# Freed activation tiles as buffers: three for gathered rows and four for weights in place of eight for weights

## The chip, the core and the metric

The kernel runs on one core of a Trainium2 chip. The metric is the device time of one execution in microseconds: 1776.36 us before the change, the median of 3 runs (1776.22 to 1776.38). A profile of one execution gives each instruction's time on the engines: PE (TensorE matmuls), PEld (its weight loads), DVE (VectorE), ACT (ScalarE), POOL (GpSimd) and SP, which issues most transfers.

## The reference

It is one layer of an encoder for two groups of tokens: 256 of a prompt and 128 (8 x 16) that are sampled, 1024 wide. A front part (modulation, projections, RWKV-7 and sparse attention, mixing) makes `x` and `h2`. What the change touches is the last part, a mixture of 16384 tiny experts:

```python
def block(hb):
    q = (hb @ w_pq).reshape(PEER_BLOCK, PEER_HEADS, 2, PEER_DHALF)
    ...
    e = jnp.take_along_axis(cidx, j, axis=-1)
    g = jax.nn.softmax(sc, axis=-1)
    act = jax.nn.gelu(jnp.einsum('nhkd,nd->nhk', peer_u[e], hb).astype(jnp.float32))
    return jnp.einsum('nhk,nhkd->nd', (g * act).astype(hb.dtype), peer_v[e])
```

For each token, 8 heads pick 16 experts each, so 128 of 16384. An expert is one row of `peer_u` and one row of `peer_v`, each 1024 floats. The output is `x + g2 * PEER(h2)`.

## The kernel before

The 128 sampled tokens go the **sparse** way (`peer_sparse`): one token per partition, and for each of its 128 experts one indirect DMA from POOL (L1593) gathers the rows u and v of that expert for all tokens, 128 x 2048 floats or 1 MB, into a row buffer. `ring` hands these buffers out, three of them (`EB = 3`, tag `raw`). DVE then multiplies u with h2 and sums to a dot product (L1600), ACT applies gelu and the weight (L1601, L1602), and DVE adds v times that to `acc` (L1606). The buffer is free after that.

The 256 prompt tokens go the **dense** way, over all 128 blocks of 128 experts. A key product (`dense_u`, accumulators `fx` and `mm`) makes gelu(h2 u), a tile of 128 experts x 256 tokens; for blocks 0 to 75 these stay in `G`, a tensor of 128 x 76 x 256 floats, for the others they are made during the next phase, a few ahead (`gA`) or by way of DRAM (`gO`, `gB`, L1522). They are multiplied by the routing weights (in `weights` for G, on POOL at L1528 for the others, with `Ws` from L1563). The last phase runs 128 value products (`dense_v`), numbered n from 0: each loads a 128 x 1024 block of `peer_v` (512 KB, `expert`, L1483), splits it into a high and a low part (`wh` on ACT at L233, `wl` on DVE at L237; likewise `Gh` and `Gl` for the tile of G) and adds twelve matmuls into the four accumulators `bx`, `cp`, `dx`, `dx` (L229); about every third product is done whole, without the split. Blocks below 76 and those above are interleaved by `order`.

While products run, the tiles of G that have been used are free. The kernel before appends one slot of four tiles (four tiles of 256 floats are one 1024-float weight buffer) to the queue of weight buffers after each of the blocks 3, 7, 11, ..., 31, so that it has four buffers at first and twelve at the end. Loads for key products use the same queue.

The sparse chain is drawn into this phase by `pull`: 0.62 of a gather per product, 55 gathers having been drawn in earlier phases. A gather also waits for its pace, the end of product n - 5. After product 122 what is left of the sparse chain is drawn, and the rows for the end are taken from the same ring: the gate (`gate2`, L1568, copied from a PE product) and the residual (`x1_rows`, L1581). `residual` multiplies the result by the gate and adds the residual (L1576, L1577), and L1578 stores it. It runs for the sampled tokens on `acc` and twice for the prompt on the four accumulators, after `finish_v` has done the last two products bank by bank.

The order of instructions on each engine is set by a scheduler when the program is built: it plans the program on a timeline of its own and puts the instructions of each engine in the order of that plan. On the chip each engine takes its instructions in that order, and each waits for what it reads and for the buffer that it writes.

Of the kernel before, what the change touches and what calls it, by code (L numbers as in the profile page):

```python
# [183 lines left out]
S0, PH = 30, 4  # L184
OFF = [j for j in range(NW, 128) if (j - NW + 1) * NB // (128 - NW) > (j - NW) * NB // (128 - NW)]
AHEAD = sorted(OFF + [j for j in range(NW, 128) if j not in OFF][:NA - 1])
LAST, EARLY, SLOTS = 126, 108, 8
WB, EB = (4, 4, 3), 3
UENG, VENG, GENG, VN = 'v', 'v', 'g', 3
SENG = 'gv'  # L190
# [7 lines left out]
class K:  # L198
    def __init__(self, ctx, tc, I, O):
        self.ctx, self.tc, self.nc, self.I, self.O = ctx, tc, tc.nc, I, O  # L200
        self.uid = 0
        self.const = self.open(ctx, "const")
        self.stream = self.open(ctx, "stream")
        self.dram = self.open(ctx, "dram", space=bass.MemoryType.DRAM)
        self.nlo = 0
        self.slots = deque([None] * WB[0])
        self.lo_pattern = "v"

    def open(self, ctx, name, **kw):
# [1259 lines left out]

    def ring(self):  # L1470

        r = self.t([128, 2048], tag="raw", bufs=EB, pool=self.peer)
        return r[:, :1024], r[:, 1024:]

    def expert(self, src):

        s = self.slots.popleft()
        self.slots.append(s)
        if s is None:
            w = self.t([128, 1024], tag="w", bufs=WB[0], pool=self.stream)  # L1480
        else:
            w = self.G[:, 4 * s:4 * s + 4].rearrange("p a b -> p (a b)")
        self.nc.sync.dma_start(w, src)  # L1483
        return w

# [124 lines left out]
    def run(self):  # L1610
# [79 lines left out]
        def pull(rate):  # L1690
            sn[0] += rate
            while sn[0] >= 1:
                sn[0] -= 1
                next(sparse, None)
# [46 lines left out]
        for n, j in enumerate(order):  # L1741
            self.pace = self.vdone[n - 5] if n > 4 else None
            pull(SR[2])
            while todo and sum(u not in OFF for u in gs) < NA - 1:
                u = todo.pop(0)
                gs[u] = self.dense_u(u)
            last.append(self.dense_v(j, gs.pop(j) if j >= NW else self.G[:, j], out, n))
            if j < 4 * SLOTS and j % 4 == 3:
                self.slots.append(j // 4)
            if n == 122:  # L1750
                for _ in sparse:
                    pass
                (a, b), (y, _) = self.ring(), self.ring()
                self.residual(0, [self.acc[:, c * 512:c * 512 + 512] for c in range(2)], self.gate2(0, a), self.x1_rows(0, b), y)
                (a, b), (c, y1), (y2, _) = (self.ring() for _ in range(3))
                g, x1, y = self.gate2(1, a), [self.x1_rows(1, b), self.x1_rows(2, c)], (y1, y2)
# [28 lines left out]
```

## Time and profile before

| | before |
|---|---|
| median of the runs | 1776.36 us |
| profiled execution, its time | 1775.95 us |
| its span | 1773.9 us |
| PE busy | 1664.8 us, 94% |
| DVE busy | 1354.5 us, 76% |
| gathers, POOL, L1593 | 128, 177.3 us busy, 501.9 us idle before them |
| gather, issue to landing | 8.3 us (median) |
| value products on PE | 1278 to 1718 us |
| moved in all | 437.22 MB, 246 GB/s |

The span runs from the first to the last instruction, and the execution's own time lies around it. A busy time is a sum over the span; what a stage is limited by is read from that stage. In the rows of groups, the idle time stands behind the busy time and the mean of one instruction, with the instruction that ended most of it. A row of waits names who waited, for whom, for how long in all, how many times, and the longest.

### The profile page before, as it was taken

Reading aid. Unit: us, or ns where it says so; the run is one execution under the profiler, and the core shown is the slowest. Engines: PE = TensorE matmul, PEld = TensorE weight load, DVE = VectorE, ACT = ScalarE, POOL = GpSimd, SP = SyncE. Lnnn points to the kernel's source line nnn. Section 1 sums busy time; section 2 is a strip of 40 time slices with the busy share of each in tenths; the row PEclk is TensorE's granted clock in tenths of the full one; section 3 lists DMA queues with packets and bytes.
Section 4 is the critical chain, followed back from the end, with each engine's and each line's share of the span. In section 5 each row is a group of like instructions: output and inputs, shape, how many; then the busy total and the mean of one; then the engine's idle time right before and its main releaser. Section 6 shows DMA issues by size and latency. Waiting matters only on the chain. (4 is left out here: it accounts for less than half of the span.)

```text
span 1773.9 us, 33227 instructions
## 1 busy us (share of the span) xinstructions
PE 1664.8 (94%) x12376; PEld 1412.1 (80%) x12376; DVE 1354.5 (76%) x2905; ACT 750.9 (42%) x1666; POOL 549.8 (31%) x621
## 2 busy tenths in 40 slices
PE   6999999999999988999999989999999999999970
PEld 4898788878878866998887889999876777777750
DVE  4449788878768845566999998999766676777896
ACT  4533433333333233444222365678733343434531
POOL 2434243333332310034123223431233123223332
PEclk8999999999999999999999999999999999999995
DMA  8543752463364276655598989986499989999957
GB/s 296 164 141 99 214 173 72 157 202 110 102 220 143 79 260 209 211 177 187 188 374 322 347 326 390 381 296 203 168 377 404 357 331 360 338 343 338 333 211 258
DMA packets 173049, 437.22 MB, mean 246 GB/s; under 512 B 46036, under 2 KB 86612, under 8 KB 156504
## 3 DMA queue, kind: packets, MB, share of 16 engines
q1 hardware_dynamic: 154456, 300.89, 50.2%
q0 software_dynamic: 18432, 134.23, 20.0%
q8 instruction: 97, 1.59, 0.4%
q14 instruction: 64, 0.52, 0.1%
HBM read 403.75 MB, written 31.30 MB: 245 GB/s over the span
## 5 line engine op out<-in xcount | busy, mean ns | idle before, releaser
L1593 POOL DMA_INDIRECT raw<-in_puv,pe x128 | 177.3, 1385 | 501.9 <-DVE acc L1606 319.7
L237 DVE TENSOR_TENSOR wl<-w,wh 128x1024 fp32r<-128x1024 f32 x208 | 261.1, 1260 | 91.8 <-ACT wh L233 35.3
L233 ACT ACTIVATE wh<-w 128x1024 fp32r<-128x1024 f32 x216 | 226.9, 1053 | 152.0 <-PE mm L229 71.0
L229 PE MATMUL fx<-h2h,wh 128*128 128x256 f32 x688 | 196.5, 286 | 0.2 <-ACT G L1509 0.2
L229 PE MATMUL fx<-h2h,wl 128*128 128x256 f32 x688 | 193.9, 283 | 2.1 <-DVE wl L237 2.1
L229 PE MATMUL fx<-h2l,wh 128*128 128x256 f32 x688 | 193.6, 282 | 0.0
L1606 DVE SCALAR_TENSOR_TENSOR acc<-raw,dots,acc 128x1024 f32<-128x1024 f32 x127 | 163.5, 1287 | 21.4 <-ACT dots L1602 20.6
L1600 DVE SCALAR_TENSOR_TENSOR raw<-raw,sh 128x1024 f32<-128x1024 f32 x128 | 159.8, 1249 | 15.2 <-DMA raw<-in_puv,pe 15.1
L229 PEld LDWEIGHTS fx<-h2h,wl 128*128 128x128 f32 x688 | 130.0, 189 | 3.7 <-DVE wl L237 3.1
L229 PEld LDWEIGHTS fx<-h2h,wh 128*128 128x128 f32 x688 | 129.9, 189 | 2.5 <-issue 1.2
L229 PEld LDWEIGHTS fx<-h2l,wh 128*128 128x128 f32 x688 | 129.7, 189 | 2.2 <-issue 1.7
L229 PE MATMUL mm<-LTh,wh 128*128 128x384 f32 (+2 forms) x352 | 123.7, 352 | 1.4 <-ACT wh L233 0.8
L229 PE MATMUL mm<-LTl,wh 128*128 128x384 f32 (+2 forms) x352 | 122.1, 347 | 1.4 <-POOL LTl L490 1.4
L229 PE MATMUL mm<-LTh,wl 128*128 128x384 f32 (+2 forms) x352 | 122.5, 348 | 0.0
L237 DVE TENSOR_TENSOR wl<-G,wh 128x1024 fp32r<-128x1024 f32 x66 | 84.9, 1288 | 47.3 <-issue 29.2
L1601 ACT ACTIVATE dots<-dots 128x1 f32<-128x1 f32 x128 | 25.4, 198 | 193.5 <-DVE raw L1600 193.4
L229 PE MATMUL mm<-h2f,w 128*128 128x256 f32 x464 | 105.4, 381 | 0.0
L229 PE MATMUL mm<-wh,LTh 128*128 128x256 f32 x336 | 99.0, 295 | 1.9 <-ACT qx L893 1.9
L229 PE MATMUL mm<-wl,LTh 128*128 128x256 f32 x336 | 100.0, 298 | 0.0
L229 PE MATMUL mm<-wh,LTl 128*128 128x256 f32 x336 | 98.7, 294 | 0.0
L229 PEld LDWEIGHTS mm<-h2f,w 128*128 128x128 f32 x464 | 87.5, 190 | 12.4
L229 PE MATMUL fx<-h2f,w 128*128 128x256 f32 x336 | 78.1, 385 | 0.0
(604 smaller groups left out, 4375.4 us busy)
## 6 DMA issues: line engine op xcount, KB each, us to landing
w<-in_puT SPq DMA_DIRECT2D x118, 512.0 KB, 6.7
G<-in_pv SPq DMA_DIRECT2D x74, 512.0 KB, 5.9
w<-in_w_in SPq DMA_DIRECT2D x70, 512.0 KB, 4.5
w<-in_pv SPq DMA_DIRECT2D x54, 512.0 KB, 6.2
w<-in_w_ada SPq DMA_DIRECT2D x48, 512.0 KB, 4.7
cKT<-in_cKT SPq DMA_DIRECT2D x32, 256.0 KB, 4.1
cV<-in_cV SPq DMA_DIRECT2D x32, 256.0 KB, 4.0
w<-in_w_pq SPq DMA_DIRECT2D x16, 512.0 KB, 3.7
```

The costliest lines, as they stand in the source:

```text
L229: return self.nc.tensor.matmul(out, l, r, start=start, stop=stop, skip_group_check=True, **kw)
L233: self.nc.scalar.activation(hi, src, AF.Copy)
L237: (self.nc.vector if eng == "v" else self.nc.gpsimd).tensor_tensor(lo, src, hi, op=OP.subtract)
L1593: d = nc.gpsimd.indirect_dma_start(out=bass.AP(tensor=u.tensor, offset=u.offset, ap=[u.ap[0], [1, 2048]]), out_offset=None, in_=self.I["puv"],
L1600: nc.vector.scalar_tensor_tensor(u, u, 1.0, h2, op0=OP.mult, op1=OP.mult, accum_out=dot)
L1601: nc.scalar.activation(dot, dot, AF.Gelu_apprx_tanh)
L1606: nc.vector.scalar_tensor_tensor(acc, v, dot, acc, op0=OP.mult, op1=OP.add)
```

## The change

A table `FREED` says after which block which tiles of G become free, and as what. The letters are taken in turn: R is a row buffer of eight tiles (2048 floats), W is a weight buffer of four. So after block 7 tiles 0 to 7 become a fourth row buffer, after block 11 tiles 8 to 11 a fifth weight buffer, after 19 the next row buffer (12 to 19), then 23 (W), 31 (R), 35 (W) and 39 (W). In the order of the value products these are numbers 9, 16, 30, 36, 50, 57 and 63. At the end there are six row buffers (before: three) and eight weight buffers (before: twelve). `ring` hands out its buffers from a queue, as `expert` did already.

```diff
-LAST, EARLY, SLOTS = 126, 108, 8
+LAST, EARLY = 126, 108
+FREED = {}
+for _k in "RWRWRWW":
+    _a = max((j + 1 for j in FREED), default=0)
+    FREED[_a + (7 if _k == "R" else 3)] = (_k, _a)
...
         self.slots = deque([None] * WB[0])
+        self.rslots = deque([None] * EB)
...
     def ring(self):
 
-        r = self.t([128, 2048], tag="raw", bufs=EB, pool=self.peer)
+        s = self.rslots.popleft()
+        self.rslots.append(s)
+        if s is None:
+            r = self.t([128, 2048], tag="raw", bufs=EB, pool=self.peer)
+        else:
+            r = self.G[:, s:s + 8].rearrange("p a b -> p (a b)")
         return r[:, :1024], r[:, 1024:]
...
-            w = self.G[:, 4 * s:4 * s + 4].rearrange("p a b -> p (a b)")
+            w = self.G[:, s:s + 4].rearrange("p a b -> p (a b)")
...
-            if j < 4 * SLOTS and j % 4 == 3:
-                self.slots.append(j // 4)
+            if j in FREED:
+                kind, a = FREED[j]
+                (self.slots if kind == "W" else self.rslots).append(a)
```

The buffers move the scheduler's plan, and so the order on the engines. The lines of the new kernel are 5 to 11 higher: its gather is at L1603, the dot product at L1610, the accumulation at L1616, the split at L242. A name's number grows in the order in which the program makes its tiles, so that a small number beside a large one is work drawn early and done late. A tile in G carries the number of G itself; its dot product then tells which gather it is.

POOL, in the middle of the phase, where gathers (L1593) stand among the multiplications of key tiles by routing weights (L1528), before:

```order
L1593 DMA raw_16925<-in_puv,pe_2107_10741 128x2048
L1593 DMA raw_16991<-in_puv,pe_2107_10741 128x2048
L1528 TENSOR_TENSOR gA_17118<-gA_17118,Ws_17931 128x256
L1528 TENSOR_TENSOR gA_17257<-gA_17257,Ws_17931 128x256
L1593 DMA raw_17020<-in_puv,pe_2107_10741 128x2048
L1528 TENSOR_TENSOR gB_17659<-gB_17659,Ws_17661 128x256
```

and now, around the same multiplications:

```order
L1603 DMA raw_17376<-in_puv,pe_2107_10741 128x2048
L1603 DMA raw_17409<-in_puv,pe_2107_10741 128x2048
L1603 DMA raw_17443<-in_puv,pe_2107_10741 128x2048
L1538 TENSOR_TENSOR gA_17127<-gA_17127,Ws_17936 128x256
L1538 TENSOR_TENSOR gA_17264<-gA_17264,Ws_17936 128x256
L1603 DMA G_11076<-in_puv,pe_2107_10741 128x2048
L1538 TENSOR_TENSOR gB_17666<-gB_17666,Ws_17668 128x256
```

Ahead of the same tile gB there stood gather 17020, and there stands now one after 17443: gathers are planned some 13 products earlier against the dense work.

DVE, early in the phase, dot products (L1600) and splits (L237) before:

```order
L1600 SCALAR_TENSOR_TENSOR raw_15768,dots_15770<-raw_15768,sh_2289_11699 128x1024
L237 TENSOR_TENSOR wl_15928<-w_15924,wh_15927 128x1024
L1606 SCALAR_TENSOR_TENSOR acc_11701<-raw_15768,dots_15770,acc_11701 128x1024
L237 TENSOR_TENSOR wl_15972<-G_11076,wh_15971 128x1024
L237 TENSOR_TENSOR Gl_16003<-G_11076,Gh_16002 128x256
```

and now:

```order
L1610 SCALAR_TENSOR_TENSOR raw_15966,dots_15968<-raw_15966,sh_2289_11699 128x1024
L242 TENSOR_TENSOR wl_16003<-w_16000,wh_16002 128x1024
L1616 SCALAR_TENSOR_TENSOR acc_11701<-raw_15966,dots_15968,acc_11701 128x1024
L242 TENSOR_TENSOR wl_16040<-w_16036,wh_16039 128x1024
L242 TENSOR_TENSOR Gl_16103<-G_11076,Gh_16102 128x256
```

A dot product stood 158 numbers ahead of the split behind it, five products; it now stands beside the split of the product with which it was drawn. Later in the phase the distance before grows to 31 products, and now it is two to five.

DVE, at the end of the phase, around the last splits, before:

```order
L237 TENSOR_TENSOR wl_18754<-G_11076,wh_18753 128x1024
L237 TENSOR_TENSOR Gl_18761<-gB_18757,Gh_18760 128x256
L1606 SCALAR_TENSOR_TENSOR acc_11701<-raw_17979,dots_17981,acc_11701 128x1024
L1600 SCALAR_TENSOR_TENSOR raw_18046,dots_18048<-raw_18046,sh_2289_11699 128x1024
L1606 SCALAR_TENSOR_TENSOR acc_11701<-raw_18046,dots_18048,acc_11701 128x1024
```

and now:

```order
L1610 SCALAR_TENSOR_TENSOR G_11076,dots_18511<-G_11076,sh_2289_11699 128x1024
L242 TENSOR_TENSOR Gl_18683<-gA_17894,Gh_18682 128x256
L242 TENSOR_TENSOR wl_18606<-w_18603,wh_18605 128x1024
L1616 SCALAR_TENSOR_TENSOR acc_11701<-G_11076,dots_18511,acc_11701 128x1024
L1586 TENSOR_TENSOR G_11076<-acc_11701,G_11076 128x512 x2
L242 TENSOR_TENSOR wl_18631<-w_18628,wh_18630 128x1024
```

Before, the last split (18754) had 13 more dot products behind it. Now the dot product of the last gather (18511, drawn with product 117) stands ahead of the last seven splits, and its accumulation and the sampled tokens' residual (L1586) ahead of six.

## The prediction

> **What bounds the kernel now.** I read the table by stages first, over the last 488 us, in which the value products run (columns: PE, PEld, DVE, ACT and POOL busy us, granted clock, DMA share, GB/s).
>
> ```profile
> 1286.00:1320.00 34.00, 34.00 (x156) 25.93 (x155) 21.17 (x26) 12.70 (x25) 14.92 (x16) 1.00 0.99 370
> 1320.00:1360.00 40.00, 38.57 (x163) 26.88 (x162) 30.51 (x37) 16.57 (x32) 12.29 (x10) 1.00 1.03 404
> 1360.00:1400.00 40.00, 40.00 (x190) 30.40 (x189) 27.23 (x35) 15.79 (x31) 9.31 (x9) 1.00 0.96 361
> 1400.00:1500.00 100.00, 100.00 (x441) 72.51 (x439) 69.23 (x82) 39.89 (x76) 26.02 (x24) 1.00 0.94 353
> 1500.00:1600.00 100.00, 100.00 (x445) 73.36 (x444) 70.86 (x82) 39.68 (x75) 30.95 (x25) 1.00 0.94 338
> 1600.00:1700.00 100.00, 100.00 (x422) 75.65 (x421) 83.02 (x99) 47.73 (x87) 35.39 (x25) 1.00 0.84 308
> 1700.00:1718.00 18.00, 18.00 (x77) 14.09 (x76) 16.60 (x21) 6.41 (x15) 6.05 (x5) 1.00 0.65 232
> 1718.00:1754.00 36.00, 0.29 (x2) 0.00 (x0) 25.39 (x31) 5.44 (x21) 14.54 (x10) 0.54 0.83 293
> ```
>
> Up to 1718 us PE is full, at full clock, and the transfers nearly so. Then PE is empty for 36 us. The rows of time show its first value product, its last, what ends the pause, and the last adds and stores.
>
> ```profile
> 1278.13 2.81 PE L229 MATMUL bx<-w,G 128*128 128x512 f32 x6
> 1717.90 0.39 PE L229 MATMUL dx<-wh,Gl 128*128 128x512 f32 x1
> 1754.18 3.78 PE L229 MATMUL fx<-modr,clate 128*128 128x512 f32 x4 [35.89 <-ACT raw L1568]
> 1767.06 1.29 DVE L1576 TENSOR_TENSOR raw<-dx,raw 128x512 f32<-128x512 f32 x2
> 1769.13 1.29 DVE L1577 TENSOR_TENSOR raw<-raw,raw 128x512 f32<-128x512 f32 x2 [0.77 <-DMA raw<-d]
> ```
>
> The chain of waits over that tail is made of gathers:
>
> ```profile
> 1717.96 10.36 DMA raw<-in_puv,pe x2
> 1728.76 8.23 DMA raw<-in_puv,pe
> 1737.08 6.58 DMA raw<-in_puv,pe
> 1750.65 6.45 DMA raw<-in_puv,pe
> 1759.67 1.30 DVE acc L1606
> 1765.15 3.88 DMA raw<-d
> ```
>
> The issues between 1718 and 1758 us and, from the waits between 1286 and 1700 us, why they come so late:
>
> ```profile
> raw<-in_puv,pe POOLq DMA_INDIRECT x10, 6.3
> ...
> POOL raw L1593 <- DVE acc L1606: 191.9, 35, 9.7
> POOL raw L1593 <- PE dx L229: 42.8, 9, 6.9
> PE bx L229 <- ACT wh L233: 1.0, 1, 1.0
> ```
>
> Ten of the 128 gathers are issued after PE's last product. While PE worked, POOL stood 191.9 us because none of three row buffers was free, against 42.8 us for the pace (product n-5). PE itself waited 1.0 us. So two limits share the end: PE to 1718.3 us (1717.90 + 0.39), then a sparse chain that is late for want of buffers.
>
> **The change part by part.** *Arithmetic.* No product, gather or load is added, and no duration should move: what is a buffer in G is 128 partitions of the same size as before. Cost 0.
>
> *Three more row buffers.* They remove the wait on acc. In the new order the dot product of a gather stands beside the split of the weights pulled with it, and the last accumulation stands ahead of the last splits; before it stood behind them. The tail of gathers then lies beside PE's work. If PE isn't slowed, what stands behind its last product is one multiplication, one addition and the store. The first two are 1.29 / 2 each by the two DVE rows; the add ends at 1769.13 + 1.29 = 1770.42 and the span at 1773.9, so the store and the close take 3.5 us. With 0.3 us for hand-overs (chosen, below the gap of 0.77 us in the last row) the tail is 0.65 + 0.65 + 3.5 + 0.3 = 5.1 us. The lower end of the span is 1718.3 + 5.1 = 1723.4 us. The gate and residual rows for it were also late (3.88 us for raw<-d) because they use the same buffers; the new order has them ahead of the last splits, covered by the same products. Without that cover, 3.9 us more.
>
> *What the transfers must carry.* This is the term that decides. By the table, 370 x 34 + 404 x 40 + 361 x 40 + 353 x 100 + 338 x 100 + 308 x 100 + 232 x 18 + 293 x 36 us make 158 MB from 1286 us to the last gather. About 2 MB of it (four loads of 512 KB) may follow the last gather, so 156 MB must have moved before it. In the new order the dot product of the last gather (pulled with product 117) stands ahead of the split of product 121, so seven products follow it. A product is twelve matmuls at 0.227 us, two such halves:
>
> ```profile
> 1701.57 1.36 PE dx L229 x6
> 1706.03 1.38 PE dx L229 x6
> ```
>
> that is 2.72 us, 19 us for seven, and 3 us for the dot product and the split between landing and PE. PE's end is thus the later of 1718.3 and 1286 + 156 MB / rate + 22 us:
> - at 404 GB/s, reached for 40 us in 1320:1360, the last gather lands at 1672 us: PE isn't slowed;
> - at 345 GB/s, the mean of 1400 to 1600 us as it is, 452 us: PE ends at 1760, slowed by 42 us;
> - at 368 GB/s, the same 345 divided by its share of 0.94, 424 us: PE ends at 1732, slowed by 14 us.
>
> I take the third: three more requests in flight fill the idle 6%, and these are the rows of the same mix of loads. The ends stay for the range. The pause in 1320:1360 gives the same size by another way: PE lost 1.4 of 40 us with the queues full, which over 390 us of full queues is 14 us.
>
> The Trainium skill, "DMA: Bandwidth & Descriptors", section "Specifications", gives about 358 GB/s of HBM per core. By that, an estimate from its figure, PE would end at 1744 us, 26 us slowed, and the kernel at 1752. The row with 404 GB/s over 40 us disagrees with it as a ceiling, so it stays inside my range.
>
> *Four weight buffers fewer at the end, eight in place of twelve in all, and later.* The fifth comes after product 16 (before: 3), the eighth after 63. With four, the fp32 key products before 1020 us kept PE at 96 to 97% full at 3.0 us a load:
>
> ```profile
> 800.00:900.00 100.00, 97.60 (x572) 85.79 (x572) 87.08 (x399) 35.42 (x72) 28.83 (x27) 0.98 0.62 210
> 900.00:1000.00 100.00, 96.48 (x451) 84.13 (x450) 98.60 (x382) 30.75 (x81) 27.85 (x24) 0.97 0.92 349
> ```
>
> A value product takes (1718.3 - 1278.1) / 128 = 3.4 us with the key products between, so four buffers cost at most 3.5% of the 55 us to product 16, 2 us. That is the upper end; the lower is 0, as the first loads now queue behind fewer others. I count it within the 14.
>
> **The sum.** 1718.3 + 14 + 5.1 = 1737.4 us of span. The profiled execution has 1775.95 us for a span of 1773.9, 2.05 around it, and the median of the runs is 0.41 above that execution: 1737.4 + 2.05 + 0.41 = 1740 us.
>
> **The rivals.** *A: the transfers go no faster than before.* The 345 GB/s could be what this mix gives. For it: share 0.94 already, and landing times in the crowded stretch (below). Against it: 404 GB/s. PE ends at 1760, the kernel at 1760 + 5.1 + 2.5 = 1768 us.
>
> *B: weights starve.* From the issues of 1286:1320, 1320:1350 and the queues of 1320:1360 and 1300:1700:
>
> ```profile
> w<-in_pv SPq DMA_DIRECT2D x7, 512.0 KB, 11.2
> raw<-in_puv,pe POOLq DMA_INDIRECT x6, 9.2
> ...
> G<-in_pv SPq DMA_DIRECT2D x4, 512.0 KB, 13.2
> ...
> q1 hardware_dynamic: 3521, 8.78, 57.7%
> q0 software_dynamic: 1008, 7.34, 44.8%
> ...
> q1 hardware_dynamic: 34477, 81.02, 55.4%
> q0 software_dynamic: 7856, 57.15, 37.2%
> ```
>
> Gathers move as packets of 57.15 MB / 7856 = 7.3 KB, the rest as 2.35 KB. If a full gather queue took half of the packets, it would take 76% of the bytes, some 303 of 400 GB/s, and leave 97 where 81.02 MB / 400 us = 203 are needed. Each 1.05 MB gather would then set PE back by 3.46 us x 106 / 203 = 1.8 us where no loads are ahead: 22 gathers to product 36 (0.62 a product, at most five weight buffers), 40 us, and the kernel at 1780. Against it: in 1320:1360 with both queues full the gathers had 7.34 of 16.1 MB, 45%, and PE lost 1.4 us. The Trainium skill, same page, section "Queues, rings and completion order", says that an engine goes round its queues packet by packet; the 45% is less than that rule would give, though three buffers may not have kept the queue full.
>
> *C, the slower side: the dot products hold up the splits.* DVE takes its work in order. The new order puts the dot product of a gather pulled with product n right ahead of the split of product n to n+2 (before, up to 31 products later), and the gather may not start before product n-5 is done. From the groups between 1286 and 1718 us:
>
> ```profile
> L1606 DVE SCALAR_TENSOR_TENSOR acc<-raw,dots,acc 128x1024 f32<-128x1024 f32 x58 | 74.7, 1287 | 14.9 <-ACT dots L1602 14.5
> L1600 DVE SCALAR_TENSOR_TENSOR raw<-raw,sh 128x1024 f32<-128x1024 f32 x58 | 73.9, 1274 | 0.5 <-DMA raw<-in_puv,pe 0.5
> L237 DVE TENSOR_TENSOR wl<-w,wh 128x1024 fp32r<-128x1024 f32 x44 | 57.4, 1304 | 30.8 <-PE dx L229 10.7 <-ACT wh L233 10.2 <-issue 6.9
> ```
>
> Where the split is that of product n, landing, dot product (1.27), split (1.30) and some 0.5 of hand-over must fit into four products, 13.8 us, so landing may take 10.7 us. The gathers' 9.2 us fits; the weights' 13.2 us would not. At a landing of 14 us each round of four products loses 3.3 us, 58 / 4 = 14.5 rounds up to product 58 lose 48, and the kernel ends at 1740 + 48 = 1788 us. It decides from 13.2 us on (36 us of gain / 14.5 rounds = 2.5 us). Behind the waiting dot product on DVE stand split and Gl of the next product, and PE waits for both. Against it: DVE waited 0.5 us for gathers at L1600, with the queues as full as in the second row.
>
> *D: the gathers aren't earlier.* If the pace were the limit, buffers would change nothing: 1776 us. For it are the 42.8 us, against it the 191.9.
>
> **How the numbers follow.** Forecast 0.73 (1740; its own range 1725 to 1758), A 0.13 (1768), B 0.04 (1780), C 0.06 (1788), D 0.04 (1776). The range 1725 to 1770 holds the forecast's cases but for its edges, and A. A measurement of this kernel tells 0.2%, 3.6 us, from no change. Faster: forecast and A, 0.86. Slower: B and C, 0.10. Same: D, 0.04.
>
> **What would show it.** Right: PE's pause of 35.89 us is gone, the last gather is issued before PE's last product, POOL's wait on acc falls far below 191.9 us, and the DMA share between 1400 and 1700 us rises to 0.97 or more. The 14 us would stand as waits of PE or of ACT and DVE on w, G or raw loads. PE's end at 1718 means the transfers had room to spare; one at 1745 or later with a share still near 0.94 means A; weight landings above 13 us with waits of wh on loads in the first 100 us mean B; a large wait of L1610 (L1600 before) on its gather, with PE waiting for wl, means C. The prediction is wrong if PE's value products end after 1750 us, or if a new wait stands behind their end.

## The result, and the profile after

| | before | after |
|---|---|---|
| median of the runs | 1776.37 us (6 runs, 1772.91 to 1777.25) | 1747.84 us (6 runs, 1745.32 to 1751.29) |
| profiled execution, its span | 1775.95, 1773.9 us | 1751.29, 1749.5 us |
| value products, first start to last end | 1278.1 to 1718.3 us, 440.2 | 1280.7 to 1744.7 us, 463.9 |
| last product to the end of the span | 55.6 us | 4.8 us |

The time after is 0.9842 of that before (95% interval 0.9828 to 0.9857), 28 us less. The forecast was 1740. The profiled execution is the slowest of the six, so sums made against it stand 3.5 us above the median.

The stages of the changed kernel (columns as in the first rows of the prediction):

```profile
1286.00:1320.00 34.00, 32.74 (x144) 23.22 (x142) 16.64 (x23) 10.52 (x22) 13.97 (x14) 1.00 0.93 346
1320.00:1360.00 40.00, 35.77 (x151) 24.29 (x151) 32.27 (x37) 16.04 (x33) 15.74 (x11) 1.00 0.96 365
1360.00:1400.00 40.00, 40.00 (x173) 28.80 (x171) 32.18 (x38) 16.06 (x32) 12.26 (x10) 1.00 1.01 381
1400.00:1500.00 100.00, 98.82 (x437) 71.68 (x436) 79.57 (x94) 38.89 (x81) 38.03 (x30) 1.00 1.00 381
1500.00:1600.00 100.00, 99.40 (x441) 72.59 (x440) 77.93 (x91) 39.15 (x81) 31.24 (x26) 1.00 1.00 385
1600.00:1700.00 100.00, 96.88 (x397) 68.59 (x395) 80.56 (x96) 41.67 (x84) 37.02 (x30) 1.00 0.98 376
1700.00:1718.00 18.00, 16.22 (x64) 12.62 (x63) 16.83 (x22) 8.85 (x18) 1.18 (x1) 0.91 0.77 267
1718.00:1735.00 17.00, 14.12 (x59) 10.39 (x58) 15.37 (x17) 8.82 (x16) 4.77 (x3) 1.00 0.15 58
...
1280.74:1744.68 463.94, 448.31 (x1913) 322.68 (x1912) 358.32 (x421) 183.48 (x371) 155.59 (x126) 1.00 0.92 349
```

The transfers are full from 1360 to 1700 us, at 376 to 385 GB/s where they had 308 to 361, and almost done by 1718, where before they ran on to the end. PE is no longer quite full: it was idle 2.0 of 440.2 us, and is idle 463.94 - 448.31 = 15.6 us. By the rows, 5.5 us of that lie between 1286 and 1360 us, only 1.8 us in the 240 us from 1360 to 1600 with full transfers, 3.1 us in the next 100, and 4.7 us between 1700 and 1735, where the transfers run out (a share of 0.77, then 0.15). Its busy time is 10 us longer too.

The rows of time, with the last gather, its dot product, the last value product and the last addition:

```profile
1280.74 2.81 PE L234 MATMUL bx<-w,G 128*128 128x512 f32 x6
1693.07 0.94 POOL L1603 DMA_INDIRECT G<-in_puv,pe  x1 [1.66 <-PE dx L234]
1720.49 1.22 DVE L1610 SCALAR_TENSOR_TENSOR G<-G,sh 128x1024 f32<-128x1024 f32 x1
1744.29 0.39 PE L234 MATMUL dx<-wh,Gl 128*128 128x512 f32 x1
1745.44 0.69 DVE L1587 TENSOR_TENSOR raw<-raw,raw 128x512 f32<-128x512 f32 x1
```

The pause of 35.89 us is gone, and the last gather is issued 51.6 us ahead of PE's end, where ten were issued behind it. The waits of POOL, of PE and of DVE's dot products during the value products:

```profile
POOL raw L1603 <- PE dx L234: 110.0, 31, 8.7
POOL G L1603 <- PE dx L234: 62.8, 18, 6.4
POOL G L1603 <- DVE acc L1616: 20.3, 5, 6.5
...
PE bx L234 <- ACT wh L238: 7.9, 8, 1.8
PE bx L234 <- DVE wl L242: 3.6, 4, 1.7
PE bx L234 <- DMA w<-in_pv: 1.7, 1, 1.7
...
DVE raw L1610 <- DMA raw<-in_puv,pe: 0.5, 1, 0.5
```

POOL's wait for a buffer (acc) fell from 204.2 us over the same stage (191.9 from 1286 to 1700 us) to 20.3, and its wait for the pace rose from 42.8 to 172.8. Further waits of its gathers are put down to other instructions of DVE (splits and dot products): 31.4 us now, 5.9 before. PE now waits for splits, 11.5 us in these rows and 1.5 us in the key products between, against 1.4 us before.

### The profile page after: what moved, and what is told of

Read it like the earlier page. It is cut to its first block, busy times and chain, and to the rows that moved or that the text cites. A ratio compares the mean times of both kernels' runs of the same rounds, so it can differ in the third digit from the quotient of the medians.

```text
span 1749.5 us, 33109 instructions
## 1 busy us (share of the span) xinstructions
PE 1671.5 (96%) x12376; PEld 1411.1 (81%) x12376; DVE 1358.9 (78%) x2905; ACT 744.2 (43%) x1666; POOL 550.2 (31%) x621
## 4 chain that ended last, share of the span: by engine, by line
PE 63%; DVE 17%; DMA 8%; issue 6%; ACT 3%; POOL 2%; SPq 0%; DVEq 0%; POOLq 0%; ACTq 0%
PE mm L234 23%; PE fx L234 12%; PE dx L234 11%; PE cp L234 7%; PE bx L234 7%; DVE acc L1616 2%; DVE wl L242 2%; DMA raw<-in_puv,pe 2%; DVE raw L1610 2%; DMA w<-in_w_in 1%; ACT wh L238 1%; DMA w<-in_puT 1%; POOL raw L1603 1%; DMA w<-in_pv 1%; DVE ps L1331 1%
## 5 line engine op out<-in xcount | busy, mean ns | idle before, releaser
L242 DVE TENSOR_TENSOR wl<-w,wh 128x1024 fp32r<-128x1024 f32 x231 | 291.5, 1266 | 94.3 <-ACT wh L238 55.3
L238 ACT ACTIVATE wh<-w 128x1024 fp32r<-128x1024 f32 x239 | 250.3, 1051 | 156.7 <-PE mm L234 70.9
L1603 POOL DMA_INDIRECT raw<-in_puv,pe x100 | 136.0, 1360 | 335.9 <-DVE acc L1616 118.0
L1616 DVE SCALAR_TENSOR_TENSOR acc<-raw,dots,acc 128x1024 f32<-128x1024 f32 x99 | 129.4, 1307 | 8.6 <-ACT dots L1612 8.5
L1610 DVE SCALAR_TENSOR_TENSOR raw<-raw,sh 128x1024 f32<-128x1024 f32 x100 | 125.4, 1254 | 7.4 <-DMA raw<-in_puv,pe 7.2
L234 PEld LDWEIGHTS mm<-LTh,wh 128*128 128x128 f32 (+2 forms) x352 | 66.7, 189 | 7.6 <-ACT wh L238 2.9
```

Source lines behind the costliest of these rows:

```text
L234: return self.nc.tensor.matmul(out, l, r, start=start, stop=stop, skip_group_check=True, **kw)
L238: self.nc.scalar.activation(hi, src, AF.Copy)
L242: (self.nc.vector if eng == "v" else self.nc.gpsimd).tensor_tensor(lo, src, hi, op=OP.subtract)
L1603: d = nc.gpsimd.indirect_dma_start(out=bass.AP(tensor=u.tensor, offset=u.offset, ap=[u.ap[0], [1, 2048]]), out_offset=None, in_=self.I["puv"],
L1610: nc.vector.scalar_tensor_tensor(u, u, 1.0, h2, op0=OP.mult, op1=OP.mult, accum_out=dot)
L1616: nc.vector.scalar_tensor_tensor(acc, v, dot, acc, op0=OP.mult, op1=OP.add)
```

## The experiments

Each kernel is the changed one with one edit, timed beside the kernel before on the same chip. Ratios are to that, with 95% intervals.

### The two halves apart

*Row buffers alone* and *weight buffers alone*: one kind is dropped from the table.

```diff
+FREED = {j: f for j, f in FREED.items() if f[0] == "R"}   # rows only
+FREED = {j: f for j, f in FREED.items() if f[0] == "W"}   # weights only
```

> The three row buffers stay, the four freed weight buffers are left unused: four weight buffers all through, as before product 16. Row theory (the gain is the tail of gathers that moves beside PE): the pause of 36 us stays away, so the time is clearly below 1776. If PE's loss of some 24 us in the value products comes from crowded transfers that make loads late, it must grow when only four loads can be ahead: 1758 to 1772 us. If it comes from the order on DVE and ACT at the start and at the end instead, four buffers suffice and it stays at 1746 to 1755.

> The four weight buffers stay, the three row buffers are left unused. Row theory: the gathers wait for acc again, the pause of 36 us on PE comes back and the time is 1774 to 1778 us, as before, with eight weight buffers in place of twelve. Rival (the gain came from the smaller lead of the weights, which left transfers to the gathers): a good part of it stays, 1750 to 1765 us.

Rows alone: 1753.44 us (1750.90 to 1756.24), ratio 0.9869 [0.9843, 0.9896]. Weights alone: 1763.92 us (1757.43 to 1768.16), ratio 0.9916 [0.9886, 0.9945]. The second has three row buffers, as before, and four weight buffers in place of eight, and yet gains 12 us. In its profile the pause (a row of time) and POOL's wait on acc are smaller, not gone (53.2 us more are put down to splits):

```profile
1748.37 3.78 PE L235 MATMUL fx<-modr,clate 128*128 128x512 f32 x4 [16.31 <-ACT raw L1579]
```

```profile
POOL raw L1604 <- DVE acc L1617: 121.8, 24, 12.0
POOL raw L1604 <- PE dx L235: 99.9, 24, 9.9
```

Fewer weight buffers alone had shortened a wait that I had put down to the number of row buffers. So the next run gave G's tiles to nobody.

*No added buffer at all*: four weight and three row buffers all through.

```diff
-for _k in "RWRWRWW":
-    _a = max((j + 1 for j in FREED), default=0)
-    FREED[_a + (7 if _k == "R" else 3)] = (_k, _a)
```

> No tile of G is used as a buffer: four weight and three row buffers all through. The kernel with four freed weight buffers and no row buffer took 1764 us, 12 less than before with eight of them. If a smaller lead of the weights is what leaves transfers to the gathers, this is as fast or faster, 1758 to 1765 us. If some lead is needed to keep PE fed, it is slower, 1766 to 1775; if that kernel's gain had another cause, 1776.

1755.40 us (1750.39 to 1763.87), ratio 0.9885 [0.9854, 0.9917]: 18 us below the kernel before (1773.83 on that chip), by taking eight buffers away and giving none. Its waits over the value products:

```profile
POOL raw L1600 <- PE dx L231: 158.2, 43, 9.8
...
POOL raw L1600 <- DVE acc L1613: 8.8, 2, 5.2
```

With the same three row buffers the wait on acc is 8.8 us in place of 204.2. Even with the 40.9 us that are put down to DVE's splits it is a quarter of that. The buffers weren't few; the accumulation that frees them came late. Nor did fewer loads let the gathers land sooner. From 1300 to 1700 us, before and without added buffers:

```profile
raw<-in_puv,pe POOLq DMA_INDIRECT x54, 8.2
...
raw<-in_puv,pe POOLq DMA_INDIRECT x66, 8.7
```

The interval of this run just touches that of the change (0.9828 to 0.9857), so what the change's own seven buffers add, 8 us by the medians, is barely told from nothing.

### Row buffers added to the kernel before

Why it came late is in the order of DVE's instructions. The names' numbers in the built programs tell with which product a dot product was drawn, and with which the last split of weights (wl) ahead of it. Their difference, in products, is the table's third column (median and largest of the phase); a negative one means that the dot product stands ahead of splits of earlier products. In the last two columns are the value stage and PE's pause behind it, of the profiled executions (of which those without any added buffer, weights only and rows added were the slowest of their runs, 4 to 8.5 us above the median).

| buffers added | ratio | dot product behind, median, largest | dots behind the last such split | value stage | pause |
|---|---|---|---|---|---|
| 8 W early (before) | 1 | 17, 31 | 13 | 440.2 us | 35.9 us |
| 8 W early, then 3 R | 0.9919 | 17, 30 | 13 | 446.8 | 8.4 |
| 4 W | 0.9916 | 3.5, 21 | 8 | 447.5 | 16.3 |
| RWRWWWWWW | 0.9842 | 3, 15 | 3 | 454.2 | 1.1 |
| RWRWRWWWWWW | 0.9857 | 2, 11 | 0 | 462.8 | none |
| RWRWRWW (after) | 0.9842 | 1, 4 | 0 | 463.9 | none |
| 3 R | 0.9869 | -1, 1 | 0 | 466.0 | none |
| none | 0.9885 | -1, 1 | 0 | 474.4 | none |

Two theories now stood against each other. *Buffers*: three more of them let POOL run ahead. *Order*: in the scheduler's plan more weight buffers let the dense work run ahead of the sparse chain, so that the dot products are written behind the splits of far later products. On the chip DVE keeps that order, and POOL's wait for a buffer follows from it. Row buffers given late change the first and not the second:

```diff
-for _k in "RWRWRWW":
+for _k in "WWWWWWWWRRR":
```

> The kernel before with its eight early weight buffers, and then three row buffers from the tiles behind them (WWWWWWWWRRR). By the theory of the prediction, want of row buffers, the three make up for lateness once they come, after product 63: PE's pause falls from 36 us to 10 or less and the time to 1750 to 1758. By the rival, that the weights' lead in the plan places the dot products late on DVE: the order still has them 20 to 24 products behind from there on and 13 behind the last split, so the pause stays at 30 us or more and the time at 1768 to 1778.

1763.41 us (1758.19 to 1768.52), ratio 0.9919 [0.9894, 0.9944], between the two expectations. Its profile, with a fourth row buffer from product 63 on, a fifth from 76 and a sixth from 90: the waits, the last stage and the times at the end.

```profile
POOL raw L1603 <- DVE acc L1616: 201.2, 35, 9.7
...
POOL G L1603 <- DVE acc L1616: 17.3, 7, 4.7
```

```profile
1700.00:1735.00 35.00, 28.04 (x112) 22.09 (x110) 34.89 (x44) 13.44 (x33) 15.99 (x12) 0.90 0.58 206
```

```profile
1740.23 3.56 PE L234 MATMUL fx<-modr,clate 128*128 128x512 f32 x4 [8.37 <-ACT G L1578]
1741.41 1.56 POOL L1603 DMA_INDIRECT G<-in_puv,pe  x1 [1.15 <-DMA G<-in_puv,pe]
```

The wait on acc is as large as before (201.2 + 17.3 us). As the buffers come late, the part from 1590 us on, about when the sixth comes, says more: 89.9 us with them, 85.6 before. What the buffers bring stands at the end: gathers there overlap, DVE is busy 34.89 of 35 us where it had gaps, and 12 of the 28 us are gained. The rest is the order's: 13 dot products and 13 accumulations behind the last split are 13 x (1.25 + 1.31) = 33 us of DVE by the groups' means, which the added buffers don't remove:

```profile
L1616 DVE SCALAR_TENSOR_TENSOR acc<-raw,dots,acc 128x1024 f32<-128x1024 f32 x57 | 74.7, 1310 | 11.2 <-ACT dots L1612 10.0 <-ACT dots L1611 0.7
L1610 DVE SCALAR_TENSOR_TENSOR raw<-raw,sh 128x1024 f32<-128x1024 f32 x57 | 71.4, 1254 | 0.0
```

Neither theory was right alone. In the old order three more buffers, given from product 63 on, are worth 12 us. The other 16, by difference, come with the change of order. No run changes the order and nothing else, and none has early row buffers in the old order.

*Two row buffers and seven for weights*, which put the dot products later again:

```diff
-for _k in "RWRWRWW":
+for _k in "RWRWWWWWW":
```

> Two row buffers and seven weight buffers (RWRWWWWWW). The dot products stand 3 to 8 products behind for most of the phase and 13 at the end, three of them behind the last split. If a later place of the sparse work frees the splits and costs only what is left at the end, the value stage is 455 us, a pause of 5 to 8 us follows, and the time is 1746 to 1752, no different from the changed kernel. If the third row buffer is needed as such, 1756 or more.

1749.19 us (1745.55 to 1749.76), ratio 0.9842 [0.9822, 0.9862], the same as the change. The third row buffer isn't needed as such. The value stage is shorter, 454 us, as PE waits 1.6 us for wh where it waited 7.9, and what is gained there goes into the end.

*Four more weight buffers behind the change's seven* (RWRWRWWWWWW):

```diff
-for _k in "RWRWRWW":
+for _k in "RWRWRWWWWWW":
```

> The change and four more freed weight buffers behind it (tiles 40 to 55, after products 70 to 90), so that there are six row and twelve weight buffers at the end. If PE's loss comes from loads that are late for want of buffers, the end gets better: 1742 to 1746 us. If the transfers are full anyway, nothing: 1746 to 1750. If a longer lead of the weights takes them from the gathers, worse: 1751 to 1758.

1749.89 us (1744.37 to 1751.28), ratio 0.9857 [0.9831, 0.9883]. Eight weight buffers cost nothing where the row buffers come first. The kernel before has the same twelve weight buffers in all and takes 1776, but it has them earlier (after products 3 to 49, here 16 to 90), so the two don't show the worth of row buffers alone. Between no added buffer (0.9885) and rows alone (0.9869) nothing can be told.

*A weight buffer first*:

```diff
-for _k in "RWRWRWW":
+for _k in "WRWRWRW":
```

> The same three row and four weight buffers in another order: the first freed tiles are a weight buffer, after product 3, and the row buffers come after products 16, 36 and 57 in place of 9, 30 and 50. If the 5 us that PE lost up to 1360 us are for want of weight buffers, they come back: 1741 to 1744 us. If they are the crowded queues, or if the later row buffers put the gathers behind, 1747 to 1752 us.

1753.06 us (1752.68 to 1756.01), ratio 0.9872 [0.9848, 0.9897]. Its stages:

```profile
1320.00:1360.00 40.00, 38.98 (x167) 27.56 (x165) 32.48 (x38) 15.33 (x32) 16.86 (x13) 1.00 1.01 392
1360.00:1400.00 40.00, 35.89 (x152) 25.99 (x151) 29.49 (x36) 15.14 (x32) 10.92 (x9) 0.96 0.94 356
```

PE's idle time of 1320 to 1360 us falls from 4.2 to 1.0 us, and 4.1 us appear in the next 40. PE's early loss isn't one late load that a buffer would mend.

### What makes the value products 24 us longer

The prediction gave 14 us to the transfers. *Half the bytes of a gather*: only the row v is fetched, and h2 stands in for v in the sum, so the sampled tokens' result is another one and u isn't read.

```diff
-    ... ap=[u.ap[0], [1, 2048]]), in_=self.I["puv"],
+    ... ap=[u.ap[0], [1, 1024]]), in_=self.I["pv"],
-    nc.vector.scalar_tensor_tensor(acc, v, dot, acc, ...)
+    nc.vector.scalar_tensor_tensor(acc, h2, dot, acc, ...)
```

> The changed kernel with half of each gather: only the v rows are fetched (0.5 MB in place of 1 MB), they are used in the dot product in place of u, and h2 in the accumulation in place of v, so the sampled tokens' result is another one. Instructions and their lengths on DVE, ACT, POOL and PE stay. The transfers of the value products fall from about 159 to 122 MB. If PE's loss of some 20 us there (460 against 440 us) is the crowding of the transfers, it goes: value products 440 to 444 us and the time 1722 to 1732 us. If it is the order on DVE and ACT (dot products ahead of splits), it stays: 455 us or more, 1740 to 1748.

1811.97 us (1807.01 to 1818.29), ratio 1.0225 [1.0193, 1.0258]: slower, against all that was expected. Waits from 1000 us on, and the value stage:

```profile
PE dx L1404 <- DVE pix L1380: 63.9, 4, 45.2
```

```profile
DVE raw L1610 <- DMA raw<-in_pv,pe: 43.2, 17, 7.4
...
DVE G L1610 <- DMA G<-in_pv,pe: 19.3, 10, 3.5
```

```profile
1331.99:1800.60 468.61, 447.09 (x1906) 325.21 (x1904) 351.54 (x422) 179.78 (x371) 160.40 (x125) 0.99 0.76 270
```

Most of the loss stands ahead of the value products: shorter gathers are planned earlier. In DVE's order 58 dot products stand ahead of the end of the selection of experts (L1380), 27 in the changed kernel, and PE waits 63.9 us for that selection. The value stage is not shorter for it, 468 us, though the DMA share in it is 0.76 in place of 0.92. There DVE waited 62.5 us for gathers, 0.5 in the changed kernel. So fewer bytes didn't shorten it; as the order moved with them, the run doesn't prove that bytes play no part.

*Less work on DVE, in the same order*: in the last phase only 128 of 1024 columns are accumulated, so most of the sampled tokens' sum is left out.

```diff
+    c = 1024 if self.pace is None else 128
-    nc.vector.scalar_tensor_tensor(acc, v, dot, acc, ...)
+    nc.vector.scalar_tensor_tensor(acc[:, :c], v[:, :c], dot, acc[:, :c], ...)
```

> The changed kernel, but in the last phase the accumulation adds only 128 of 1024 columns, so that most of the sampled tokens' sum is left out; the order on the engines, the loads and the gathers stay as they are. It takes some 1.2 us from each of 73 instructions on DVE, 88 us in all, and no byte from the transfers. If the 24 us by which the value products last longer than before come from DVE, whose queue now holds the sparse work between the splits, most of them return: value stage 445 to 452 us in place of 464, 1728 to 1738 us. If the transfers set it (share 1.00 from 1360 to 1700 us), nothing moves: 1744 to 1751.

1741.87 us (1740.86 to 1745.78), ratio 0.9813 [0.979, 0.9837]. The group and the stage:

```profile
L1617 DVE SCALAR_TENSOR_TENSOR acc<-raw,dots,acc 128x128 f32<-128x128 f32 x42 | 17.3, 411 | 6.8 <-ACT dots L1612 6.8
```

```profile
1278.78:1734.70 455.92, 445.39 (x1912) 321.45 (x1912) 290.67 (x421) 181.29 (x371) 145.45 (x126) 1.00 0.93 355
```

DVE has 358.3 - 290.7 = 68 us less to do in the stage, the stage is 8 us shorter, and the time falls by 6 us (the intervals of the two ratios overlap). The accumulations are a third of the 24 us at most; neither expectation was met.

What PE does wait for can be seen late in the phase in the changed kernel, ACT and PE by time:

```profile
1721.14 0.42 ACT L238 ACTIVATE Gh<-gA 128x256 fp32r<-128x256 f32 x1 [1.88 <-PE dx L234]
1721.46 1.04 ACT L238 ACTIVATE wh<-w 128x1024 fp32r<-128x1024 f32 x1
...
1722.56 0.50 PE L234 MATMUL bx<-wh,Gh 128*128 128x512 f32 x1 [1.00 <-ACT wh L238]
```

The split of a weight stands behind a Gh that waits for PE to give its buffer back; PE then has the length of the split, 1.0 us, with nothing to do. PE has seven more waits for wh, of 0.45 to 1.8 us. In four of the eight a Gh stands ahead as here, in three a gelu that waits for its dot product (at 1345, 1553 and 1607 us), in one the gate's copy that waits for acc (at 1709). ACT stood as long on Gh before (118.7 us, 120.1 now), but PE waited for wh 1.0 us in all: then the splits were written further ahead. The waits of ACT ahead of a split of weights, before and now, show it:

```profile
ACT wh L233 <- PE fx L229: 27.2, 11, 4.8
...
ACT wh L238 <- DMA w<-in_puT: 12.1, 5, 6.1
ACT wh L238 <- DMA w<-in_pv: 5.7, 4, 3.0
```

Before, ACT stood 27.2 us until PE was done with an older product, which I read as a wait for a buffer of wh. Now that wait is gone, and those for loads are 17.8 us (13.5 before). In the table above the stage is longer the less the dot products are behind, which fits, but I have no run that changes the place of the splits and nothing else.

### Limits that could have taken over

*Gathers issued earlier in the program* (the rates of `pull` for the last two phases), *a looser pace* (the end of product n - 9), and *the buffers of the end rows taken from G's tiles 40 to 71* in place of the ring:

```diff
-SR, UR = (0.5, 0.5, 0.62), 0.5
+SR, UR = (0.5, 0.6, 0.56), 0.5                              # earlier gathers
-self.pace = self.vdone[n - 5] if n > 4 else None
+self.pace = self.vdone[n - 9] if n > 8 else None            # looser pace
-(a, b), (y, _) = self.ring(), self.ring()                   # end rows
+a, b, y, a2, b2, c, y1, y2 = (self.G[:, 40 + 4 * k:44 + 4 * k] ... for k in range(8))
```

> The change with the gathers drawn at 0.60 in place of 0.50 per step while the routing weights are made (where the transfers are busy for 0.46 to 0.6 of the time), and at 0.56 in place of 0.62 per value product: some six gathers, 6 MB, leave the crowded stretch. If crowded transfers cost PE its 20 us, each MB less gives up to 2.6 us there: 1733 to 1742 us. If DVE, full at 96% in that earlier stretch, is held up by the extra sums instead, what is won is lost ahead of the value products: 1748 to 1758.

> The changed kernel, with the pace at the end of product n - 9 in place of n - 5. POOL's waits for PE (173 us) move. If the pace now bounds the kernel, the sparse chain ends earlier and the time falls to 1738 to 1743. If not, since DVE waited for gathers 0.5 us only, the time is 1745 to 1752. If a dot product that stands closer to its gather holds up the splits (rival C; the order now has them 1 to 4 products ahead of their split), 1753 to 1762.

> The gate, residual and result rows of the end get tiles 40 to 71 of G, used by product 117, in place of places in the ring of row buffers, so that they wait for no accumulation. In the changed kernel the last 94 us of work took 12 us longer than before. If that is the ring (a gate copy on ACT that waited 2.2 us for acc with a split behind it), most comes back: 1737 to 1743 us. If the last dot products and accumulations on DVE are what holds up the splits, little changes: 1745 to 1750 us. If it's the transfers, nothing: 1748 us.

Earlier gathers: 1751.13 us (1747.03 to 1753.56), ratio 0.9864 [0.9839, 0.9888]. The looser pace: 1752.97 us (1750.31 to 1759.11), ratio 0.9877 [0.9849, 0.9905]. The end rows: 1747.58 us (1743.54 to 1749.64), ratio 0.984 [0.9816, 0.9863]. None is faster than the change; the looser pace lies at the border of two expectations, which it doesn't tell apart. Earlier gathers met the second expectation. With six gathers fewer in it, their value stage is shorter, and it starts later, at 1296.4 us in place of 1280.7:

```profile
1296.41:1745.82 449.41, 441.48 (x1904) 322.03 (x1902) 336.95 (x402) 177.88 (x356) 139.98 (x120) 1.00 0.91 346
```

With its last matmul that is 449.8 us, 14 less than in the change, or 2.3 us for each gather, and 16 us were lost ahead of it. Against the kernel before, the change runs 12 more dot products within the stage, and it is 24 us longer, 2.0 us each. So a gather moved under the products takes about 2 us from PE (an estimate from these two); whether by its transfer or by its work on DVE and ACT, these runs don't tell.

With the looser pace POOL still waits for PE, as each gather is issued further ahead:

```profile
POOL raw L1603 <- PE dx L234: 96.3, 27, 8.0
POOL G L1603 <- PE dx L234: 85.0, 21, 7.9
```

These 181 us, like the 172.8 of the change, cost nothing that shows: in the change DVE waited for gathers 0.5 us in the whole stage, and the gather issued last, at 1693 us, had its dot product at 1720, 27 us later, three times the 9.2 us to landing of the crowded stretch before. The pace is a long wait without a price.

## Why the prediction was right, and where it wasn't

**Sum.** The forecast span was 1737.4, the profiled one is 1749.5. The first value product starts 2.6 us later, the stage is 463.9 - 440.2 = 23.7 us longer where 14 were given, and the tail is 4.8 where 5.1 were. 2.6 + 9.7 - 0.3 = 12.0, of which 3.9 fall away in the median, since the profiled run of before lay 0.4 below its own and this one 3.5 above. That is the 8 us between 1740 and 1748. That it is no more is partly luck, as the 14 us stood for something that cost PE little (below).

**What bounds the kernel: right.** PE to 1718 us and then a late sparse chain. All that was to show it came: no pause, the last gather ahead of PE's end, a small wait on acc, a share of 0.98 or more.

**"Late for want of buffers": half right.** The row said `POOL raw L1593 <- DVE acc L1606`, and I took it for too few buffers. It names what gave the buffer back; that instruction came late, as its dot product stood 17 products back at the median, up to 31, in DVE's order. Three row buffers are enough when the order is another (8.8 us of that wait without added buffers, 49.7 with the waits put down to splits), and more of them, given late, don't shorten it when the order stays (218 us). Quoting the order of before, with a distance that grows to 31 products, I had the cause in hand and used it only for rival C.

**"Four weight buffers fewer: 0 to 2 us": wrong in sign.** Their absence moved the plan, and taking all eight away is worth 18 us alone. The rule that a buffer fewer can only cost holds for a fixed order, and here the order is made from the buffers.

**The slip of 14 us: 24 in the profiled run, and not by the way given.** The volume was right: the rows of the table from 1286 to 1700 us make 156 MB. The rate over these 414 us was 376 GB/s where I took 368, and by my own formula PE then ends at 1286 + 414 + 22 = 1722 us, slowed by 4. It ended at 1744.7. The step that failed is that the landing of the last gather sets PE's end. Its dot product waited in DVE's order until 1720, and PE had lost most of its time already. Of the 24 us, 13.6 are idle time (the listed waits for splits grew by 11.6 us, a wait for a load is 1.7), 2.0 are four gate products that used to stand behind the stage, about 2 are the slower clock described below, and some 6 of PE's longer busy time I haven't traced. The other way to the 14 us, 1.4 of 40 us lost at full queues, fails as well: from 1360 to 1600 us PE lost 1.8 us in 240.

The Trainium skill, "DMA: Bandwidth & Descriptors", section "Specifications", has about 358 GB/s per core; by that the prediction had PE's end at 1744 and the kernel at 1752. The times come close, but the trace doesn't bear out the way: 376 to 385 GB/s over 340 us, and the last gather issued at 1693.

**The rivals.** A (no faster than 345 GB/s) and D (the pace) are out by the rows above. B, weights starving, is out as I described it: PE waited 1.7 us for a load directly, and a weight buffer put first brought nothing; a part by way of ACT's waits for loads (17.8 us) isn't excluded. C, dot products that wait for their gathers and hold up the splits, is out for the change, where L1610 waited 0.5 us for gathers, but DVE does wait so with half rows: 62.5 us. A milder form is in the change: three of PE's eight waits for wh stand behind a gelu that waits for its dot product. The chance of 0.10 on the slower side rested on a real mechanism, one order away.

**Still open:** of the 24 us, what the splits' place, DVE's work (6 us) and full transfers each take. The value stage grows as the pause shrinks nearly all through the table, and no version that leaves no work out has a median below 1747 us.

## What to carry to other kernels

A wait for a buffer names the instruction that gave it back; ask why that came late before adding buffers, and look where it stands in its engine's order. Where a scheduler makes the order from the buffers, each buffer also moves instructions: a run with no buffer added separates that from the buffer's own worth, and here it gave 18 of the 28 us, with fewer buffers than before. A cut in work (half the bytes) can lose time in the same way, so read where in the program the loss stands.

## What the runs showed of the hardware

Transfers went faster than any stretch of that length before had shown. In the kernel with two row buffers, for 100 us at 405 GB/s:

```profile
1400.00:1500.00 100.00, 100.00 (x446) 73.40 (x445) 79.42 (x94) 41.07 (x83) 36.49 (x29) 1.00 1.03 405
```

The best of before was 404 over 40 us and 353 over 100. PE was 100.00 busy there, so full queues alone don't slow it.

In the changed kernel, a short pause of PE (1.78 us) was followed by 4 us at a lower granted clock:

```profile
1710.00:1715.00 5.00, 3.49 (x9) 2.72 (x10) 4.08 (x7) 3.62 (x7) 0.00 (x0) 0.67 0.64 184
```

```profile
1711.51 0.66 PE L234 MATMUL bx<-wh,Gh 128*128 128x512 f32 x1 [1.78 <-ACT wh L238]
1711.97 0.63 PE L234 MATMUL cp<-wh,Gh 128*128 128x512 f32 x1
...
1715.95 0.39 PE L234 MATMUL bx<-wh,Gh 128*128 128x512 f32 x1
```

Some ten matmuls take 0.63 us in place of 0.39 and follow each other after 0.42 us in place of 0.23 (2.72 us for twelve): about 2 us more, as much as the pause itself. Pauses of 1.0 us showed no such dip (the clock was 1.00 from 1720 to 1725), and neither did the pause of 1.73 us at 1728.56, so the length alone doesn't decide it; what does isn't shown.
